# A hybrid attention block on eight cores: a build-time list scheduler in place of program order, fixed rings and stage barriers

## The chip, the cores and the metric

One Trainium2 chip, eight cores, two dies of four cores each. The program runs on all eight at once; every core takes two of the sixteen batch elements, so no core talks to another. The metric is device time in microseconds (us) of the slowest core. The executions here fall in two states: fast, or slow, when the cores of one die (or both) show a lower granted TensorE clock and the time is longer.

## The reference, cut to what matters

One transformer layer over 2048 latent tokens and 256 context tokens, width 1024. Its pieces, in the order in which data flow:

```python
# D=1024, SEQ=2048, CTX=256, batch 16 (2 per core), one layer
sh1, sc1, g1, sh2, sc2, g2 = adaln(c, w_ada, b_ada)      # silu(c) @ w_ada: 1024 x 6144, fp32, 24 MB
hc = modulate(rms_norm(ctx), sh1c, sc1c)                 # "norm 1", context tokens
hx = modulate(rms_norm(x),   sh1,  sc1)                  #           latent tokens
# one combined input projection, cut into q, k, v | gla q, k, v, gate | low-rank decays | merge gates
# softmax attention: 8 query heads, 2 KV heads, QK-norm, rotary; 2304 keys
attn = softmax(q k^T) v
# gated linear attention (GLA): 4 heads, dk=128, dv=256, forward and backward scan
#   S_t = diag(a_t) S_{t-1} + k_t^T v_t ;  o_t = q_t S_t   (chunked; the kernels use chunks of 128)
gla = rms_norm(o_fwd + o_bwd) * silu(gate)
x = x + g1 * (sigmoid(ga) * (attn @ wA) + sigmoid(gb) * (gla @ wG)) @ w_out   # merge, output projection
x = x + g2 * swiglu(modulate(rms_norm(x), sh2, sc2))                          # norm 2, FFN, d_ff 2816
```

GLA and attention both read `hx` and don't depend on each other. The two batch elements of a core are independent throughout. Within a batch element, the FFN of one group of 512 tokens needs nothing of the other groups. This is the freedom that the change sets out to use.

## The kernel before

The kernel issues its instructions in program order. A small class follows who wrote and read each tile and puts the semaphore waits in; stages are walled off by barriers, and buffers come from fixed rings.

```python
def barrier(self):                       # every engine waits for all engines and all DMAs
    sps = [(E.sem, E.cnt) for E in self.E.values() if E.cnt > 0]
    sps += [(o.dsem, o.dcnt) for o in self.dsems]
    for E in self.E.values():
        for sem, val in sps:
            ...
            E.h.wait_ge(sem, val)

class Ring:                              # buffer i of n, in turn
    def next(self):
        it = self.items[self.i % len(self.items)]
        self.i += 1
        return it

# --- stage order, for each of the two batch elements (cut) ---
# adaLN (once) | norm 1 | 4 GLA heads, one after the other | K, V | 32 attention tiles | merge
#              | output projection + norm 2 | FFN, two halves of 1024 tokens      -- S.barrier() between stages
```

One GLA head is projections first, scan after. The forward scan's step, per chunk of 128 tokens:

```python
def core(n):
    S.op("act", lambda e: e.copy(out=Sbf, in_=s32_), ...)
    def mmo(e):                                          # four matmuls per chunk
        e.matmul(pso[:, 0:256], lhsT=qeT[:, 0, tok], rhs=Sbf, start=True, stop=False)
        e.matmul(pso[:, 0:256], lhsT=ATs[:, 0, tok], rhs=gv[:, i, :], start=False, stop=False)
        e.matmul(pso[:, 0:256], lhsT=qeT[:, 1, tok], rhs=SBst[:, n, :], start=False, stop=False)
        return e.matmul(pso[:, 0:256], lhsT=ATs[:, 1, tok], rhs=gv[:, i, :], start=False, stop=True)
    if n < 15:
        state_step(i, 0, first=False)                    # line 828: the state's matmul, then DVE
    S.op("pe", mmo, ...)                                 # lines 861 to 864
def norm(n):
    ...                                                  # Square, Ln, Exp on ACT; scale on DVE (line 877)
    def trs(e):                                          # lines 882, 883: fp32 transposes
        e.transpose(pst[:, 0:128], go[:, 0:128], ident)
        return e.transpose(pst[:, 128:256], go[:, 128:256], ident)
for n in range(18):
    if n < 16: core(n)
    if 0 <= n - 1 < 16: norm(n - 1)
    if 0 <= n - 2 < 16: evac(n - 2)
```

An attention tile (one head, 512 queries) runs nine pairs of key blocks: two score matmuls of 512 columns into a pair of PSUM banks, one Exp of 1024 columns on ACT, eight matmuls with V of 129 columns into an accumulator of two banks. At its end:

```python
pTv = pO2.bitcast(BF16).rearrange("p (a b) -> p a b", a=4)[:, :, 384:512]   # inside the accumulator's banks
S.op("dve", lambda e: e.reciprocal(out=rz, in_=pOv[:, :, 128]), ...)
S.op("dve", lambda e: e.tensor_tensor(out=on, in0=pOv[:, :, 0:128], in1=rz..., op=ALU.mult), ...)
def fin():
    S.op("pe", trs, reads=[on_k, cst_k], writes=pO2_k)                      # four transposes into pTv
    S.op("dve", lambda e: e.tensor_copy(out=aoT[...], in_=pTv), reads=pO2_k, ...)
```

## Time and profile before

| | before |
|---|---|
| time, median of 15 runs | 3715.21 us (3709.83 to 4145.19) |
| PE busy, mean granted clock (profiled core) | 85%, 0.935 |
| stage windows in which PE is far from full, batch 0 | start 195 us; GLA 476; K and V 72; attention 384; output projection with norm 2 110; batch 1's norm 63 |
| stage windows in which PE is full | merge 223; FFN 462 |

The page's line on the chain that ended last (the work followed back from the last instruction to whatever released it) gives PE 73% of the span; all the rest is time in which the end of the program depends on something else than a matmul.

```profile
PE 73%; ACT 7%; DVE 7%; issue 7%; DMA 4%; DVEq 0%; SPq 0%; ACTq 0%; POOLq 0%; POOL 0%
```

Three windows of the stages that the prediction rests on and doesn't show; the columns are start:end, then span, busy time and count for PE, PEld, DVE, ACT, POOL, granted clock, DMA share, GB/s.

```profile
195.00:671.00 476.00, 366.37 (x2956) 251.42 (x2976) 253.40 (x520) 241.00 (x636) 7.25 (x13) 0.88 0.10 15
671.00:743.00 72.00, 46.94 (x262) 27.36 (x268) 37.83 (x61) 23.84 (x46) 2.13 (x4) 0.88 0.20 44
743.00:1127.00 384.00, 335.21 (x3202) 219.20 (x3262) 153.08 (x250) 318.17 (x378) 3.17 (x6) 1.00 0.03 6
```

They are the four GLA heads, K and V, and attention of batch 0. In the first two no engine is above 77%, and the clock granted to TensorE is 0.88, where attention has 1.00: in these windows the emptier stages also have the lower clock. In attention ACT stands at 318 of 384 us.

### The profile page before, as it was taken

What the parts mean: (1) busy time and instruction counts of PE and PEld (TensorE: products, weight loads), DVE (VectorE), ACT (ScalarE), POOL (GpSimd) and SP (SyncE); (2) the same over time, 40 slices, a digit from 0 to 9 for tenths busy, and PEclk for the clock granted to TensorE, in tenths of its full rate; (3) what the DMA queues carried; (4) which work ended last, traced back from release to release, by engine and by line L of the source; (5) the groups of instructions that cost most, each with busy time, mean ns of one, the idle gap of its engine ahead of it and who ended that gap; (6) DMA issues with size and microseconds to landing.
All of it is one profiled execution on the core that took longest, in us unless ns stands there. A gap on an engine that the chain in (4) does not pass through costs nothing.

```text
span 3708.8 us, 58054 instructions; the slowest of 8 cores (3686.3 to 3708.8 us)
## 1 busy us (share of the span) xinstructions
PE 3144.1 (85%) x20290; PEld 1735.4 (47%) x20606; DVE 1407.9 (38%) x2448; ACT 1504.7 (41%) x2696; POOL 207.3 (6%) x382
## 2 busy tenths in 40 slices
PE   7587778688889977999977777868888998799999
PEld 1265445355554433444435455534555443344444
DVE  0244565544342334222224565554444232512212
ACT  0335555388882114101104554547888411411010
POOL 0000000000000001201100000000000000121110
PEclk9698888999999998999987888989999999899999
DMA  9401110100002246844442111010000123584452
GB/s 273 128 8 21 21 21 7 35 7 7 7 1 35 40 103 159 128 92 89 63 126 83 21 21 21 7 32 7 7 7 4 24 41 68 165 149 81 101 78 82
DMA packets 91317, 219.49 MB, mean 59 GB/s; under 512 B 8533, under 2 KB 15065, under 8 KB 89497
## 3 DMA queue, kind: packets, MB, share of 16 engines
q0 software_dynamic: 62624, 133.32, 20.3%
q1 hardware_dynamic: 28410, 82.44, 7.6%
q8 instruction: 172, 2.82, 0.3%
q14 instruction: 111, 0.91, 0.1%
HBM read 281.92 MB, written 33.55 MB: 85 GB/s over the span
## 4 chain that ended last, share of the span: by engine, by line
PE 73%; ACT 7%; DVE 7%; issue 7%; DMA 4%; DVEq 0%; SPq 0%; ACTq 0%; POOLq 0%; POOL 0%
PE ps L1270 8%; PE ps L1277 8%; PE ps L1299 8%; PE ps L1154 6%; PE ps L1147 6%; PE ps L1045 5%; PE ps L1072 5%; PE ps L939 4%; ACT sb_arenaB L1056 4%; PE ps L738 4%; PE ps L751 3%; PE ps L772 3%; PE ps L1210 3%; DVE sb_arenaB L836 2%; PE ps L410 2%
## 5 line engine op out<-in xcount | busy, mean ns | idle before, releaser
L1056 ACT ACTIVATE sb_arenaB<-ps 128x1024 bf16<-128x1024 f32 x576 | 564.5, 1028 | 9.0 <-PE ps L1045 8.1
L1072 PEld LDWEIGHTS ps<-sb_arenaB 128*128 128x128 bf16 x4608 | 302.4, 97 | 167.0 <-issue 45.3
L1045 PE MATMUL ps<-sb_arenaB 128*128 128x512 bf16 x1026 | 314.3, 378 | 77.7 <-ACT sb_arenaB L1056 72.0
L1072 PE MATMUL ps<-sb_arenaB 128*128 128x129 bf16 x4608 | 354.5, 220 | 16.2 <-DVE sb_arenaA L1093 15.6
L1281 ACT ACTIVATE sb_arenaB<-ps 128x512 f32<-128x512 f32 x176 | 105.1, 597 | 647.4 <-PE ps L1270 647.4
L1270 PE MATMUL ps<-sb_hxT,sb_wbuf 128*128 128x512 bf16 x1376 | 332.4, 382 | 9.6 <-issue 8.1
L1277 PE MATMUL ps<-sb_hxT,sb_wbuf 128*128 128x512 bf16 x1382 | 331.2, 380 | 1.4
L1282 DVE TENSOR_TENSOR sb_arenaA<-ps,sb_arenaB 128x512 bf16<-128x512 f32 x176 | 121.8, 692 | 509.4 <-PE ps L1277 494.5
L1299 PE MATMUL ps<-sb_arenaB,sb_arenaA 128*128 128x512 bf16 x1380 | 303.1, 379 | 1.5
L1147 PE MATMUL ps<-sb_hxT,sb_wbuf 128*128 128x512 bf16 x1000 | 240.4, 380 | 3.6 <-DVE sb_arenaA L1093 2.4
L1154 PE MATMUL ps<-sb_arenaA,sb_wbuf 128*128 128x512 bf16 x1006 | 241.2, 381 | 0.9
L1159 ACT ACTIVATE sb_arenaB<-ps 128x512 f32<-128x512 f32 x128 | 76.4, 597 | 358.6 <-PE ps L1147 244.9
L1270 PEld LDWEIGHTS ps<-sb_hxT,sb_wbuf 128*128 128x128 bf16 x1408 | 138.1, 98 | 175.5 <-issue 11.1
L1277 PEld LDWEIGHTS ps<-sb_hxT,sb_wbuf 128*128 128x128 bf16 x1408 | 137.9, 98 | 167.3 <-issue 1.8
L1299 PEld LDWEIGHTS ps<-sb_arenaB,sb_arenaA 128*128 128x128 bf16 x1408 | 137.6, 98 | 166.3
L836 DVE SCALAR_TENSOR_TENSOR sb_arenaB<-sb_arenaB,ps 128x256 f32<-128x256 f32 x256 | 122.8, 481 | 104.0 <-PE ps L828 80.9
L508 PE MATMUL ps<-sb_ident_bf,sb_arenaB 128*128 128x128 bf16 x544 | 61.1, 288 | 115.0 <-DVE sb_arenaB L494 85.7
L1154 PEld LDWEIGHTS ps<-sb_arenaA,sb_wbuf 128*128 128x128 bf16 x1024 | 100.4, 98 | 122.0 <-issue 2.0
L1147 PEld LDWEIGHTS ps<-sb_hxT,sb_wbuf 128*128 128x128 bf16 x1024 | 100.0, 98 | 122.9 <-issue 2.6
L939 PE MATMUL ps<-sb_hxT,sb_wbuf 128*128 128x512 bf16 x630 | 155.9, 393 | 1.0 <-issue 0.7
L968 DVE TENSOR_TENSOR sb_arenaB<-sb_arenaB 128x512 bf16<-128x512 f32 (+1 forms) x84 | 57.1, 679 | 223.8 <-ACT sb_arenaB L967 222.8
L828 PE MATMUL ps<-sb_arenaB,sb_arenaA 128*128 128x256 bf16 x272 | 93.4, 349 | 44.5 <-DVE sb_arenaB L836 37.0
(161 smaller groups left out, 4188.1 us busy)
## 6 DMA issues: line engine op xcount, KB each, us to landing
sb_wbuf<-wfi POOLq DMA_DIRECT2D x176, 256.0 KB, 4.9
out<-sb_arenaA POOLq DMA_DIRECT2D x64, 512.0 KB, 5.0
sb_arenaA<-w_ada SPq DMA_DIRECT2D x12, 2048.0 KB, 18.1
sb_wbuf<-wb POOLq DMA_DIRECT2D x68, 256.0 KB, 3.9
sb_arenaB<-x SPq DMA_DIRECT2D x32, 512.0 KB, 9.4
sb_arenaA<-x SPq DMA_DIRECT2D x32, 512.0 KB, 5.7
sb_arenaA<-out SPq DMA_DIRECT2D x32, 512.0 KB, 4.2
sb_arenaB<-wfo POOLq DMA_DIRECT2D x22, 512.0 KB, 8.3
```

The lines of the kernel that those rows point to most:

```text
L738: last = e.matmul(ps[:, k * 256:(k + 1) * 256], lhsT=hsrc(i0 + k, kt)[0], rhs=wa[:, kt, 128:384], start=(kt == 0), stop=(kt == KT - 1))
L836: S.op("dve", lambda e: e.scalar_tensor_tensor(out=new, in0=old, scalar=dlx[:, dr, i:i + 1], in1=pu[:, 0:256], op0=ALU.mult, op1=ALU.add), ...
L939: last = e.matmul(ps[:, 0:nn], lhsT=w[:, kt, :], rhs=rhs, start=(kt == 0), stop=(kt == KT - 1))
L1045: last = e.matmul(pS[:, u * 512:(u + 1) * 512], lhsT=kT[:, gg, j * 128:(j + 1) * 128], rhs=qTx, start=True, stop=True)
L1056: S.op("act", lambda e, pS=pS, PT=PT: e.activation(out=PT, in_=pS, func=AF.Exp, scale=ATT_SCALE, bias=-ATT_SHIFT), reads=pS_k, writes=[PT_k])
L1072: last = e.matmul(pOv[:, qt, 0:129], lhsT=PT[:, u * 512 + qt * 128:u * 512 + (qt + 1) * 128], rhs=Vt[:, 2 * j + g, 0:129], start=(j == 0 a ...
L1147: last = e.matmul(pG, lhsT=wg[:, kt, :], rhs=hxT[:, kt, c * 512:(c + 1) * 512], start=(kt == 0), stop=(kt == KT - 1))
L1154: last = e.matmul(pY, lhsT=wy[:, kt, :], rhs=src[:, kt, c * 512:(c + 1) * 512], start=(kt == 0), stop=(kt == KT - 1))
L1270: last = e.matmul(pA, lhsT=wa_j[:, kt, :], rhs=hxT[:, kt, c * 512:(c + 1) * 512], start=(kt == 0), stop=(kt == KT - 1))
L1277: last = e.matmul(pB, lhsT=wb_j[:, kt, :], rhs=hxT[:, kt, c * 512:(c + 1) * 512], start=(kt == 0), stop=(kt == KT - 1))
L1282: S.op("dve", lambda e, pB=pB, sa=sa, j=j, cl=cl: e.tensor_tensor(out=uT[:, j, cl * 512:(cl + 1) * 512], in0=pB, in1=sa, op=ALU.mult), rea ...
L1299: last = e.matmul(pF, lhsT=uT[:, j, tl * 128:(tl + 1) * 128], rhs=WoG[:, j, cc * 512:(cc + 1) * 512], start=(j == 0), stop=(j == NJ - 1))
```

## The change

Its intent is that the order of the instructions is no longer the order of the program text. Work is written as tasks (Python generators) that yield operations and requests for SBUF space, PSUM banks or conditions. When the program is built, a list scheduler with a cost model picks, again and again, the ready operation with the smallest (estimated start + priority), and takes buffers from one 184 KB arena and eight PSUM banks as they come free. On the chip nothing is dynamic: each engine still runs one fixed sequence. At the same time the arithmetic of adaLN and of GLA is reorganised. The diff has 1325 added and 1118 removed lines; its core, with cuts marked `...`:

```diff
-    def barrier(self):
-        sps = [(E.sem, E.cnt) for E in self.E.values() if E.cnt > 0]
 ...
+class Machine:
+    def _start(self, op):                       # alternatives (DVE or ACT for a copy): the earlier end wins
 ...
+            late = 0.0
+            if table is not None and table != E.table:
+                late = 1.3                      # price of an activation-table switch
+            if best is None or t + late + cost < best[2]:
+                best = (t, alt, t + late + cost, late)
 ...
+            self.dma_free = max(self.dma_free, E.free) + op.dma[1] / 190e3     # DMA model: 190 GB/s
 ...
+    def run(self):
 ...
+                key = max(t, self.now - 1.0) + task[0] + 0.5 * late
+                if best is None or key < best[0]:
+                    best = (key, task)

 # adaLN: 24 slices of 256 columns, outputs in four 32-partition strips
+            for kt in range(KT):
+                q = kt % 4
+                last = e.matmul(ps.ap[32 * q:32 * q + 32, 0:256], lhsT=scT.ap[:, kt, :], rhs=wa.ap[:, kt, :],
+                                start=(kt < 4 and kt > 0), stop=(kt >= 4))
 ...
+    lane([t_ada(n) for n in range(8)], 3, -2.0, "ada")
+    mod1 = lambda: ada_done[0] >= 8             # norm 1 needs only 8 of the 24
 ...
+    lane([t_ada(n, lambda n=n: att0[0] >= (n - 8) * 1.6) for n in range(8, 24)], 1, 0.3, "adb")  # under attention 0

 # GLA: a head may begin when half of the head before the last is out; no token-major K projection
+        def head_gate(h):
+            return lambda: h < 2 or out_done[h - 2] >= 4
 ...
-                        last = e.matmul(ps[:, k * 128:(k + 1) * 128], lhsT=hsrc(i, kt)[0], rhs=wa[:, kt, 0:128], ...)
+                        last = e.transpose(pv[:, dr, k * 128:(k + 1) * 128], keT.ap[:, dr, k * 128:(k + 1) * 128], ident_bf)
 ...
+                yield dve(lambda e: e.copy_predicated(out=Av, mask=maskp.ap..., data=v1), ...)   # two masked matrices into one
 ...
-                    e.matmul(pso[:, 0:256], lhsT=qeT[:, 0, tok], rhs=Sbf, start=True, stop=False)
-                    e.matmul(pso[:, 0:256], lhsT=ATs[:, 0, tok], rhs=gv[:, i, :], start=False, stop=False)
-                    e.matmul(pso[:, 0:256], lhsT=qeT[:, 1, tok], rhs=SBst[:, n, :], start=False, stop=False)
-                    return e.matmul(pso[:, 0:256], lhsT=ATs[:, 1, tok], rhs=gv[:, i, :], start=False, stop=True)
+                    e.matmul(out, lhsT=qe.ap[:, 0, o:o + 128], rhs=X["Sf"][n].ap, start=True, stop=False)
+                    e.matmul(out, lhsT=A.ap[:, o:o + 128], rhs=v.t.ap[:, n % 2, :], start=False, stop=False)
+                    last = e.matmul(out, lhsT=qe.ap[:, 1, o:o + 128], rhs=X["Sb"][n].ap, start=False, stop=True)

 # attention: the end of a tile transposes into a bank of its own
-        pTv = pO2.bitcast(BF16).rearrange("p (a b) -> p a b", a=4)[:, :, 384:512]
+            ev_fin[ti].set()                    # accumulator free: the division is done
+            pt = yield Bank(1)
+            ptv = pt.ap.bitcast(BF16)[:, 0:512]

 # FFN: a group of 512 tokens starts when its own norm 2 is done
+        def t_f(Hh, j, cl):
+            c = 2 * Hh + cl
+            yield Wait(ev_h2[c])

 # batch 1: later priority, may begin with the second half of batch 0's FFN, within a space reserve
+    g1, att0, left0 = batch(0, 0.0, lambda: True, None)      # g1: f_started >= 1
+    M.reserve = lambda: left0() + 56 * 4
+        batch(1, 3.0, g1, None)
```

## The prediction

> **What bounds the kernel now.** I read the page's head and its forty slices, then the busy times by stage, then the chain of waits inside one attention tile.
>
> The page:
>
> ```profile
> span 3708.8 us, 58054 instructions; the slowest of 8 cores (3686.3 to 3708.8 us)
> PE 3144.1 (85%) x20290; PEld 1735.4 (47%) x20606; DVE 1407.9 (38%) x2448; ACT 1504.7 (41%) x2696; POOL 207.3 (6%) x382
> ...
> PE   7587778688889977999977777868888998799999
> DVE  0244565544342334222224565554444232512212
> ACT  0335555388882114101104554547888411411010
> ...
> PEclk9698888999999998999987888989999999899999
> ```
>
> TensorE is the bound, but only in two kinds of stage (merge, FFN: nines). The low PE digits stand where ACT and DVE are high, and ACT and DVE are nearly empty where PE is full: work that could lie side by side lies one after the other. The stage windows (start:end, then span, busy time and count for PE, PEld, DVE, ACT, POOL, granted clock, DMA share, GB/s):
>
> ```profile
> 37.00:136.00 99.00, 96.50 (x230) 22.79 (x230) 9.34 (x22) 4.68 (x8) 0.00 (x0) 0.91 0.55 167
> 136.00:195.00 59.00, 15.64 (x144) 14.39 (x144) 26.04 (x49) 30.26 (x57) 1.78 (x4) 0.56 0.75 192
> 225.00:283.00 58.00, 52.14 (x437) 37.95 (x442) 29.27 (x55) 32.36 (x59) 1.60 (x3) 1.00 0.02 4
> 283.00:330.00 47.00, 26.85 (x142) 14.87 (x143) 31.91 (x73) 25.31 (x96) 0.00 (x0) 0.74 0.23 36
> 1350.00:1460.00 110.00, 74.73 (x378) 35.92 (x384) 55.01 (x81) 42.71 (x73) 10.53 (x19) 0.83 0.59 168
> 1460.00:1922.00 462.00, 455.91 (x2069) 206.97 (x2112) 105.16 (x152) 53.82 (x89) 61.52 (x112) 0.99 0.55 97
> 1922.00:1985.00 63.00, 16.15 (x144) 14.74 (x144) 27.22 (x49) 30.25 (x57) 3.73 (x7) 0.51 0.67 189
> ```
>
> These are adaLN, norm of batch 0, projections and scan of one gated-linear-attention (GLA) head, output projection with norm 2, FFN of batch 0, norm of batch 1. The FFN does 2112 matmuls of 512 columns in 462 us, hence the 0.2158 us each at which eight take 1.726 us start to start in the timeline; 256 columns take 0.110, 128 take 0.0558. I call this streaming time: the busy time counts pipeline depth too (mean 380 ns), so 85% flatters.
>
> Streaming time of one batch, counted from the loops and these three prices: norm 1 8.0; low-rank 15.6; GLA 4 x 74.4 = 298; attention's K and V 33; attention 32 x 10.2 = 326; merge 1024 x 0.2158 = 221; output projection 55 and norm 2 7; FFN 456. Sum 1420. Twice that, plus adaLN's fp32 matmuls and broadcast, about 106 (timeline: 6.96 us for eight of 512 columns, 14 us of broadcast), is 2945. So 3709 - 2945 = 764 us pass in which TensorE streams nothing. By stage: start to 195 us: 81; each GLA (476 us) 163; each K/V stage (72) 39; each attention (about 384) 58; each output projection and norm 2 (110) 48; norm of batch 1 55; small change elsewhere.
>
> Inside attention the chain of waits shows a tile of 12.1 us:
>
> ```profile
> 904.85 0.64 ACT sb_arenaB L967
> 905.49 0.92 ACT sb_arenaB L1056
> 906.42 0.35 issue
> ...
> 908.51 1.74 PE ps L939 x8
> 910.25 0.02 issue
> ...
> 910.34 0.04 ACT sb_arenaB L951
> 910.38 0.45 issue
> 910.83 1.03 ACT sb_arenaB L1056
> ```
>
> ACT has nine Exp at 0.985 us back to back (four in 3.94) plus Square 0.60, Ln 0.59 and Exp 0.64, about 10.8; PE streams 10.2. ACT binds, and loses some 1.3 us per tile at its end, where the transposes and their copy use the accumulator's own banks and hold the next PV matmuls.
>
> [...] granted clock 1.00 in dense projections, 0.74 in the scan, 0.51 and 0.56 in the norms. [...] Here the FFN ran dense on eight cores at 0.99[...], though one of the three timed runs took 4119.92 us. [...] The page here has 1283 ns on every ACT_TABLE_LOAD, so interleaving Silu with Exp and Ln has a price per switch.
>
> **The change part by part.** It replaces program order, fixed buffer rings and the barriers between stages by a list scheduler: tasks with priorities, buffers taken from one arena and PSUM banks by need, copies given to ACT or DVE, weights streamed ahead. All of it is decided when the program is built; on the chip each engine still runs one fixed order.
>
> Less streaming. Low-rank: both directions in one 64-column matmul, 15.6 to 7.8. GLA per head: token-major K projection gone (-8.0) but its context columns go through the feature-major one (+0.9); decay matmuls of one kind instead of two (-2.0); transposes of ke added (+2.0); the two masked matrices merged, so three matmuls instead of four per chunk (-1.7); output transposes bf16 instead of fp32 (-2.4). 74.4 becomes about 63.2, four heads 253. Per batch 1420 - 7.8 - 45 = 1367; both 2734. AdaLN: 24 slices of 256 columns in four strips; one unpacked fp32 256-column matmul would be 0.435, eight 3.5; [...] New streaming sum 2794, so 151 less.
>
> Less emptiness, 764 before:
> - Start. Only 8 of 24 MB of adaLN weights stand before norm 1, and x loads beside them. At the first window's 251 GB/s, 8 MB plus 3 MB of inputs is some 44 us; with latency the GLA starts near 57, not 195. The other 16 slices go under attention. Empty time 81 to 50.
> - GLA of batch 0. Scan of one head lies beside projections of the next, no ring of two. Busy demand per head: PE 63; ACT 18.9 for four fused 1024-wide Exp/Ln per chunk, 13 for 32 scaled states, 9 squares, 8 for the rest, near 49; DVE 5.4 + 5 + 5.5 + 16 + 8 + copies, near 54. Three engines at about 80% each in strict order will not reach 100%: I take 83% PE. 261 + 8 at 83% leaves 55 empty, not 163.
> - K/V: overlapped with the last scan, but attention waits for all of GLA: 10 left of 39, for each batch.
> - Attention: own bank for the transposes, so the accumulator is free after the 0.18 + 0.69 us of division. ACT floor 10.8. A 1.73 us query projection or an adaLN slice still slips in front of a score matmul. I take 11.4 us: 38 empty of 58 in each batch.
> - Output projection/norm 2: the FFN starts on the first 512 tokens while the rest is projected, no barrier and 1 MB weight wait (the chain had 17.2 us of DMA there): 12 left of 48, twice.
> - Batch 1's norm and GLA: allowed from the second half of batch 0's FFN, arena permitting. The FFN has ACT 0.12 and DVE 0.23 busy, so what fits costs only PE time. The arena reserve will hold much of GLA until the FFN's last third: 163 + 55 become 50.
> - FFN, merge, tail: about 24.
> Sum: 50 + 55 + 20 + 76 + 24 + 50 + 24 = 299. Time 2794 + 299 = 3093. Since every hole is also taken with cost guesses that look close (0.69 us for a 512-wide DVE op, as in the trace), I round towards the better side: 3075 us, 17% less.
>
> **The rivals.**
> 1. TensorE-bound all through: batch 1 vanishes under the FFN, GLA reaches 95%. For it: ACT and DVE have room on average (41%, 38%). Against: attention's ACT floor alone leaves 19 us per batch, and the start can't go. About 2930.
> 2. Order paid on the chip: greedy choice puts long PE blocks (3.5 us for a value pair or a gate pair) before short critical ones, Silu/Exp switches multiply (8 loads at one line now; 30 to 60 more at 1.3 us or so), PSUM's 8 banks stall the pipelines, weight loads queue behind POOL's copies in strict order. GLA stays at 70% and attention at 12.1: +70 +45 +60, about 3250.
> 3. [...] Against: the FFN at 0.99. I give it 5%.
> 4. Nothing hidden because DMA or the buffers bind: DMA stands at 28%, bursts of 0.8 in the FFN; batch 1 finds no arena until the FFN ends: 3150.
>
> **Range and chances.** The streaming cut (151) and the start (some 30 of emptiness) hardly depend on scheduling: 3530 already, over 2% faster. The range goes from rival 1 to rival 2 without their extremes: 2950 to 3230. Faster 0.97, same 0.02, slower 0.01.
>
> **What would show it.** First GLA matmul near 57 us; attention beginning near 400 instead of 740; tiles of 11.4 us and ACT above 90% there; scan and projections mixed, with clock above 0.95 instead of 0.88; merge 220 and FFN about 456 plus whatever batch 1 puts in between; batch 1's norm inside FFN 0 and no window at clock 0.5; PE busy above 90%. I am wrong in mechanism if those stages keep their lengths, if the batch-1 GLA runs alone at its old 476 us, or if attention lengthens under the adaLN slices; wrong in size if GLA's PE share is far from 83%.

The text is as recorded, but for passages that are cut, each marked: figures and mechanisms that no trace or run of this case shows. The sum holds a cut term: new streaming came to 2794, which is 2734 for the two batches and, for the rest, adaLN's 24 slices, whose price is cut; 2794 + 299 = 3093, put down as 3075. The 151 of less streaming, 2945 - 2794, holds that term too. At the 2.0 us of PE that a slice took under attention in the changed kernel (see below), the 24 would be 48 us and the saving 163 (an estimate); this document goes on with 151. Rival 3 said that the dense stages would run at a lower clock in most executions. The busy demands per head are estimates from counts and the mean times of like operations in the trace before (0.404 us for a scaled state, 1.05 for an activation of 1024 columns).

## The result, and the profile after

| | before | after |
|---|---|---|
| median | 3715.21 us (15 runs) | 3130.32 us (12 runs) |
| range | 3709.83 to 4145.19 | 3125.65 to 3580.81 |
| fast runs over fast runs | | 0.8421 (0.8403 to 0.8438) |

The ratio is the mean time of one kernel's fast runs over that of the other's of the same rounds, so it isn't quite the ratio of the medians. Nine of the twelve runs of the changed kernel were fast, with a mean of 3129.7 us; in the slowest, 3580.81, the cores of one die had a granted clock of 0.812 to 0.817 and those of the other 0.977 to 0.979. Below, a time of a kernel is the mean of its fast runs, and a difference is taken to 3129.7. The output is right.

The changed kernel's page: the span, the busy times, and four of the rows of forty slices.

```profile
span 3132.5 us, 55526 instructions; the slowest of 8 cores (3106.4 to 3132.5 us)
...
PE 2926.7 (93%) x19780; PEld 1649.5 (53%) x19780; DVE 1279.1 (41%) x2142; ACT 1522.0 (49%) x2436; POOL 219.4 (7%) x428
...
PE   4989879999999999999989997899999997999999
...
DVE  1565674444333452221235657644432325422222
ACT  1787768888711132101137787698883112310110
...
PEclk9999889999999999999999998999999998999999
```

Set them beside the rows in the prediction. The PE row has nines where it had fives to sevens; what is left are the start (4), the end of each batch's GLA (the first two sevens, at 392 to 470 and 1879 to 1958 us) and the output projection of batch 1 (the third, at 2584 to 2663 us, where PE is busy for 62.6 of 79 us; a wait for its weights, shown below, comes just before and reaches into it). PE's busy time fell by 217 us and DVE's by 129, ACT's rose by 17. Mean granted clock rose from 0.935 to 0.977 on the profiled cores. The chain that ended last is now

```profile
PE 83%; ACT 7%; issue 4%; DVE 3%; DMA 3%; SPq 1%; DVEq 0%; ACTq 0%; POOL 0%; POOLq 0%
```

so PE's share went from 73% to 83%. The stage windows of the changed kernel's slowest core (columns as above; the fifth is a stretch inside the third):

```profile
0.00:37.00 37.00, 5.74 (x36) 2.32 (x40) 1.77 (x9) 1.88 (x3) 5.11 (x13) 1.00 0.97 196
37.00:84.00 47.00, 32.55 (x206) 17.73 (x199) 9.93 (x24) 16.36 (x33) 0.00 (x0) 1.00 0.69 216
84.00:466.00 382.00, 332.81 (x2771) 238.72 (x2768) 239.12 (x435) 282.94 (x587) 26.64 (x63) 0.94 0.15 34
140.00:340.00 200.00, 185.72 (x1660) 140.77 (x1658) 116.48 (x214) 161.56 (x306) 17.32 (x40) 0.97 0.10 16
340.00:440.00 100.00, 77.71 (x559) 49.15 (x560) 69.04 (x138) 69.02 (x194) 4.28 (x15) 0.88 0.18 38
466.00:852.00 386.00, 378.77 (x3637) 240.94 (x3637) 163.66 (x283) 329.54 (x388) 6.35 (x12) 0.99 0.19 51
852.00:1064.00 212.00, 212.00 (x987) 96.25 (x986) 63.47 (x93) 37.93 (x63) 16.06 (x29) 1.00 0.32 48
1064.00:1198.00 134.00, 123.35 (x645) 59.55 (x644) 73.67 (x114) 48.35 (x78) 12.15 (x22) 0.96 0.67 165
1198.00:1612.00 414.00, 410.96 (x1920) 187.72 (x1919) 99.28 (x147) 55.83 (x97) 46.69 (x86) 1.00 0.54 110
1612.00:1990.00 378.00, 334.11 (x2796) 240.89 (x2793) 240.45 (x437) 287.11 (x589) 29.79 (x65) 0.93 0.15 38
1990.00:2372.00 382.00, 357.65 (x3324) 228.07 (x3325) 155.65 (x261) 332.20 (x390) 6.36 (x12) 0.99 0.06 10
...
2573.00:2720.00 147.00, 129.70 (x655) 61.24 (x654) 74.60 (x115) 48.69 (x78) 13.15 (x24) 0.93 0.73 168
```

They are: two parts of the start, GLA with K and V, the middle of GLA, the tail of the last head, attention 0, merge 0, output projection with norm 2 and the first FFN work, FFN 0, GLA with K and V of batch 1, attention 1, and the passage to the FFN of batch 1. GLA with K and V takes 382 us (378 in batch 1) and took 476 + 72 = 548. From the GLA's first projection to the start of attention, PE is busy 87% of the time and was 75% (413.31 of 548). The borders are set by eye, to some 10 us: the first score matmul of attention 1 comes only at 1999.7, and from it to PE's last work for attention pass 368 us, where the kernel before took 387 (739.4 to 1126.2). Merge, 212 and 201, is bound by streaming in both kernels (PE busy for all of the 212 and 201 us, and for 219.92 of 223 in the kernel before).

The chain in order of time, from the last long wait of the start on (start us, us, what; "DMA" is time in which the chain waits for a transfer):

```profile
22.49 30.25 DMA sb_arena<-w_ada
...
52.99 1.03 PE ps L678 x2
54.02 1.91 PE ps L682 x16
...
56.01 0.38 ACT sb_arena L583
...
56.52 0.99 PE ps L698 x4
57.51 0.99 PE ps L678 x2
58.50 1.91 PE ps L682 x16
```

GLA can't begin before adaLN's first eight slices are through. The chain waits for a slice's weights until 52.7 us; the chain has 30 us for that transfer, while x tiles and GLA weights come in beside it. Five slices are then still to be done, and they come 4.5 us apart: each is one short chain on PE, the bias's matmul (line 678, 0.99 us), the eight packed ones (line 682, 1.91), a copy on ACT, and two small fp32 matmuls that turn the result (line 698, 0.99).

The clock has a part in this that the windows hide. The trace has no clock record before 84.6 us, and the windows count time without a record as 1.00; the spacing of the matmuls says otherwise. Here are the packed eight of a slice and the 128-column bf16 transposes of norm 1 in the start, and then the packed eight of a slice under attention:

```profile
72.03 1.94 PE L682 MATMUL ps<-sb_arena,sb_scT 128*32 128x256 f32 x16
75.51 3.57 PE L756 MATMUL ps<-sb_cstb,sb_arena 128*128 128x128 bf16 x32
```

```profile
474.05 1.07 PE L682 MATMUL ps<-sb_arena,sb_scT 128*32 128x256 f32 x16
```

The transposes follow each other at 0.107 us where the prediction has 0.0558, and the same packed work takes 1.94 us instead of 1.07: until its first clock record the core runs at about half rate. Under attention the three PE steps of a slice take about 0.54 + 1.0 + 0.50 = 2.0 us, in the start 3.9, so of the 22 us that the five slices take, some 9 are the clock (an estimate from these spacings). In the kernel before, where the matmuls of adaLN are dense, the record has the full clock, 1.00, from 22.5 us on.

Two more pieces of the same chain, later:

```profile
384.12 16.75 DMA sb_arena<-wav
...
2573.16 23.61 DMA sb_arena<-wo
```

Here two weight loads hold up everything, 16.75 us before the values of attention (`wav`) and 23.61 us before batch 1's output projection (`wo`). The program lets the first begin when the last GLA head's projections are done, and the second when six of eight parts of the merge are.

### The profile page after: what moved, and what is told of

Same layout as the page of the kernel before. It is cut to its first block, busy times and chain, and to the rows that moved or that the text cites. A ratio compares the mean times of both kernels' runs of the same rounds, so it can differ in the third digit from the quotient of the medians.

```text
span 3132.5 us, 55526 instructions; the slowest of 8 cores (3106.4 to 3132.5 us)
## 1 busy us (share of the span) xinstructions
PE 2926.7 (93%) x19780; PEld 1649.5 (53%) x19780; DVE 1279.1 (41%) x2142; ACT 1522.0 (49%) x2436; POOL 219.4 (7%) x428
## 3 DMA queue, kind: packets, MB, share of 16 engines
q1 hardware_dynamic: 28784, 116.19, 11.4%
## 4 chain that ended last, share of the span: by engine, by line
PE 83%; ACT 7%; issue 4%; DVE 3%; DMA 3%; SPq 1%; DVEq 0%; ACTq 0%; POOL 0%; POOLq 0%
PE ps L1455 19%; PE ps L1485 10%; PE ps L1282 8%; PE ps L1346 7%; PE ps L1354 7%; PE ps L1308 7%; PE ps L989 4%; PE ps L893 4%; PE ps L1018 3%; PE ps L1399 3%; ACT sb_arena L1294 3%; PE ps L1223 2%; PE ps L756 1%; PE ps L1197 1%; DMA sb_arena<-w_ada 1%
## 5 line engine op out<-in xcount | busy, mean ns | idle before, releaser
L1455 PE MATMUL ps<-sb_arena 128*128 128x512 bf16 x2816 | 613.5, 379 | 0.0
L1294 ACT ACTIVATE sb_arena<-ps 128x1024 bf16<-128x1024 f32 x576 | 558.8, 1022 | 8.8 <-PE ps L1282 4.9
L1455 PEld LDWEIGHTS ps<-sb_arena 128*128 128x128 bf16 x2816 | 275.3, 98 | 331.4 <-issue 0.6
L1459 ACT ACTIVATE sb_arena<-ps 128x512 f32<-128x512 f32 x176 | 104.9, 597 | 635.1 <-PE ps L1455 635.0
L1308 PEld LDWEIGHTS ps<-sb_arena 128*128 128x128 bf16 x4608 | 303.3, 97 | 134.0 <-issue 11.8
L1282 PE MATMUL ps<-sb_arena 128*128 128x512 bf16 x1152 | 341.8, 378 | 20.2 <-ACT sb_arena L1294 15.9
L1308 PE MATMUL ps<-sb_arena 128*128 128x129 bf16 x4608 | 354.5, 220 | 3.2 <-DVE sb_arena L1243 1.5
L1485 PE MATMUL ps<-sb_arena 128*128 128x512 bf16 x1408 | 305.9, 379 | 1.0 <-DVE sb_arena L1488 1.0
L1460 DVE TENSOR_TENSOR sb_arena<-ps,sb_arena 128x512 bf16<-128x512 f32 x176 | 121.6, 691 | 426.6 <-PE ps L1455 422.3
L1358 ACT ACTIVATE sb_arena<-ps 128x512 f32<-128x512 f32 x128 | 76.4, 597 | 365.9 <-PE ps L1346 297.5
L1346 PE MATMUL ps<-sb_arena 128*128 128x512 bf16 x1024 | 241.9, 379 | 0.0
L1354 PE MATMUL ps<-sb_arena 128*128 128x512 bf16 x1024 | 241.9, 379 | 0.0
L1485 PEld LDWEIGHTS ps<-sb_arena 128*128 128x128 bf16 x1408 | 137.8, 98 | 167.7 <-issue 2.4
L1354 PEld LDWEIGHTS ps<-sb_arena 128*128 128x128 bf16 x1024 | 100.1, 98 | 120.3
L1346 PEld LDWEIGHTS ps<-sb_arena 128*128 128x128 bf16 x1024 | 100.1, 98 | 119.9
L1062 DVE SCALAR_TENSOR_TENSOR sb_arena<-sb_arena,ps 128x256 f32<-128x256 f32 x256 | 116.8, 476 | 108.7 <-PE ps L1052 102.1
L1071 ACT ACTIVATE sb_arena<-sb_arena 128x256 bf16<-128x256 f32 x256 | 124.4, 504 | 51.5 <-DVE sb_arena L1062 44.1
L989 PE MATMUL ps<-sb_arena 128*128 128x256 bf16 x1152 | 139.1, 276 | 0.0
L893 PE MATMUL ps<-sb_arena 128*128 128x512 bf16 (+1 forms) x576 | 137.8, 391 | 0.8 <-DVE sb_arena L1488 0.8
```

The lines of the kernel that those rows point to most:

```text
L893: last = e.matmul(ps.ap[:, 0:W], lhsT=w.ap[:, kt, :], rhs=hxc.ap[:, kt, :], start=(kt == 0), stop=(kt == KT - 1))
L989: last = e.matmul(ps.ap[:, k * 256:(k + 1) * 256], lhsT=hxc.ap[:, kt, o + k * 128:o + (k + 1) * 128], rhs=w.ap[:, kt, :], start=(kt == 0), ...
L1062: yield dve(lambda e: e.scalar_tensor_tensor(out=R2.ap, in0=R.ap, scalar=dl.ap[:, dr, prev:prev + 1], in1=ps.ap[:, 0:256], op0=ALU.mult, o ...
L1071: yield Op([("act", lambda e: e.activation(out=St.ap, in_=R.ap, func=AF.Copy, scale=dcol), act_cost(256, False) + 0.09, None)], [R, dl], [St])
L1282: last = e.matmul(pS.ap[:, u * 512:(u + 1) * 512], lhsT=kT[g].ap[:, j * 128:(j + 1) * 128], rhs=q.ap, start=True, stop=True)
L1294: yield act(lambda e: e.activation(out=PT.ap, in_=pS.ap, func=AF.Exp, scale=ATT_SCALE, bias=-ATT_SHIFT), act_cost(1024), [pS], writes=[PT] ...
```

## The experiments

Theory. Of the 585 us, some 151 is streaming that is no longer done; the rest is overlap in four places, each with its own wait removed (head behind head in GLA, adaLN behind attention, FFN behind norm 2, batch 1 behind FFN 0), and finer order inside the stages. Put back one of those waits and its share returns. Rival A: the overlap between stages is worth little, and the gain is streaming and the clock. Rival B: the heads hardly overlap, since three engines in strict order fill one head already. Twelve kernels ran.

### One wait put back at a time

**The heads of GLA, one after the other** (run a).

```diff
-            return lambda: h < 2 or out_done[h - 2] >= 4
+            return lambda: h < 1 or out_done[h - 1] >= 8
```

> The changed kernel, but a GLA head may only start when the one before it is finished (one gate changed). Theory A (the time came from work lying side by side): the scan and output of each head are exposed again; a head, about 86 us now for some 63 us of matmul streaming, takes 100 to 110 us, so +110 to +190 us for the eight heads, all of it between the first GLA matmul and the first score matmul of each batch. Rival B (the time came from the smaller amount of matmul work): the work is untouched, so under +20 us.

Measured: the two fast runs are 3267.8 and 3268.8 us, ratio to the kernel before 0.8797 (0.8742 to 0.8851), so 139 us more than with the change. Four of six runs were slow, the profiled one among them, on one die only:

```profile
die 0 (median of its cores): 3264.5 us, clock 0.950
die 1 (median of its cores): 3331.3 us, clock 0.926
```

The other die's median, 3264.5, is that of a fast run; only its cores were read. There each head takes about 100 us (the value projections come in bursts at 80, 200, 300 and 400 us), and attention begins at 530 instead of 466. So overlap of heads is worth about 70 us per batch. Rival B falls.

**All of adaLN ahead of norm 1** (run b).

```diff
-    lane([t_ada(n) for n in range(8)], 3, -2.0, "ada")
-    mod1 = lambda: ada_done[0] >= 8
+    lane([t_ada(n) for n in range(24)], 3, -2.0, "ada")
+    mod1 = lambda: ada_done[0] >= 24
 ...
-    lane([t_ada(n, lambda n=n: att0[0] >= (n - 8) * 1.6) for n in range(8, 24)], 1, 0.3, "adb")
```

> The changed kernel with all 24 adaLN slices before the first norm, none under attention. Theory A: 16 MB more at some 240 GB/s stand in front of the GLA, about +66 us at the start, and attention of batch 0 gets back the 20 us by which its tiles are longer than those of batch 1 (386 against 367 us): +45 us in all. Rival B: the slices cost PE and DMA wherever they lie, so under +15 us.

Measured: 3181.3, 3185.7 and 3203.1 us, ratio 0.8586 (0.8531 to 0.8640): 60 more by the mean, 56 by the median, somewhat more than expected. The expectation's 240 GB/s was an estimate; it lies between the 216 of the changed kernel's start and the 251 of the first window before. Its chain has the slices 4.5 to 6.6 us apart, all through the start, and this start too runs at about half rate, up to its first clock record at 167 us: the packed eight take 1.91 us in every slice of the chain, and 1.00 in the chain of the changed kernel under attention. There the same slice costs about 1 us in all, as will be seen below. Sixteen times the difference is 56 at least; of it some 30 are the clock (16 x 1.9 us, an estimate), and the rest falls to the holes in a slice's chain.

**The FFN waits for all of norm 2** (run c).

```diff
-            yield Wait(ev_h2[c])
+            yield Wait(lambda: all(e_.on for e_ in ev_h2))
```

> The changed kernel, but the FFN waits until all four 512-token groups have been through norm 2. Theory A: output projection and norm 2 have holes again, as in the kernel before (36 us of PE not busy in 110): +20 to +30 us for each batch, +50 in all. Rival B: under +15 us.

Measured: 3158.7, 3165.5 and 3168.8 us, ratio 0.8517 (0.8475 to 0.8559): 35 more for the two batches, and less than I expected.

**Batch 1 waits for the end of FFN 0** (run d).

```diff
-        return (lambda: f_started[0] >= 1), att_i, ...
+        return (lambda: fo_done[0] >= 16), att_i, ...
```

> The changed kernel, but batch 1 may start only when batch 0 is finished. My prediction took some 170 us of batch 1's front as hidden under batch 0's FFN; the trace shows batch 1's first transposes only at about 1580 us, 32 us before the FFN's last matmul, and the GLA of batch 1 then takes as long as that of batch 0. Theory A': the overlap that exists is worth only the norm and first loads, +20 to +40 us. Rival: the overlap does more than the trace shows, +100 us or more.

Measured: 3140.4 to 3145.3 us in four fast runs, ratio 0.8458 (0.8419 to 0.8497): 13 more. The overlap of the two batches is worth almost nothing, less than half of what I had by then come to expect.

**All four together** (run e; the edits of a, b, c and d).

> All four gates at once: heads one after the other, all adaLN first, FFN after all of norm 2, batch 1 after batch 0: the new work and buffers in the old order of stages. If the four losses are separate things they add: +135, +55, +35, +13 on 3130, about 3370. If they share holes, less: 3300. What is then left to the kernel before (about 340 us) is the 151 us of matmul streaming removed and whatever the finer order inside stages gives.

Measured: 3383.1 and 3385.3 us (four of six runs slow), ratio 0.9114 (0.9067 to 0.9161): 254 more than the change as it is. The four single costs add to 139 + 60 + 35 + 13 = 247, so they are nearly independent. What is then left, 3712.8 - 3384.2 = 329 us, is the other half of the result: the streaming that went, and order inside the stages. Three windows of this run's slowest core show where: the four GLA heads, what is left of K and V, and attention of batch 0.

```profile
170.00:578.00 408.00, 325.02 (x2597) 233.11 (x2596) 211.90 (x392) 280.75 (x540) 35.53 (x70) 0.82 0.13 31
578.00:612.00 34.00, 27.61 (x181) 16.72 (x179) 31.12 (x49) 20.42 (x45) 0.00 (x0) 1.00 0.00 1
612.00:978.00 366.00, 344.33 (x3217) 220.62 (x3216) 152.72 (x255) 321.86 (x379) 6.35 (x12) 0.99 0.06 10
```

By these windows GLA takes 408 us for 476, K and V 34 for 72, attention 366 for 384; their borders are not quite at the same places in both kernels. By the first and last matmuls of each stage, batch 0 takes from its first low-rank matmul to its first FFN matmul 133 us less (GLA with K and V 90, attention 18, output projection 29, merge 4 more), batch 1 127 less; the gap from FFN 0 to batch 1's low-rank matmuls is 30 us and was 66, and GLA begins 29 us earlier. That is 133 + 127 + 35 + 29 = 324, which covers the 329. Of it, by the prediction's count, 151 are streaming; the rest, some 180, is what is left for the order inside the stages. That is a remainder and not a measurement: only attention's accumulator was tried by itself (run h), and the clock's share was not separated. Rival A is still wrong in the main: the four overlaps alone are 254 of 585 measured us, and streaming is 151 by the count.

### The pieces inside the stages

**fp32 output transposes back in the changed kernel** (run f). The change turns two fp32 transposes per chunk into bf16 ones; I took them as pure streaming.

```diff
-            go = yield alloc([128, 2, 256], BF16, name="go")
+            go = yield alloc([128, 2, 256], F32, name="go")
 ...
-                        last = e.transpose(ptv[...], go.ap[:, u, hf * 128:(hf + 1) * 128], ident_bf)
+                        last = e.transpose(ptv[...], go.ap[:, u, hf * 128:(hf + 1) * 128], cst.ap[:, 0, :])
```

> The changed kernel with the GLA output transposed in fp32 again (256 transposes; in the trace before, the next matmul starts 0.13 and 0.11 us after one in fp32 and 0.056 us after one in bf16) and its eviction at 0.69 instead of 0.42 us. Theory (GLA of the changed kernel is matmul-bound at 79%): the 16 us of streaming cost +8 to +20 us. Rival (holes absorb it): under +4 us.

Measured: 3145.1, 3146.2 and 3146.4 us (the other four of seven were slow), ratio 0.8472 (0.8438 to 0.8506): 16 more. The trace has the loss in the right place: over all eight cores GLA with K and V takes 392 and 411 us (batch 0 and 1, first value projection to first score matmul) instead of 379 and 399, and the stages after it some 7 us less. The edit also makes the copy out of PSUM slower (0.69 us instead of 0.42 on DVE), so the matmuls alone are not shown to be the cause.

**The same piece put into the kernel before** (run g).

```diff
-        go_r = ring(2, [128, 256], F32, "go")
+        go_r = ring(2, [128, 256], BF16, "go")
 ...
-                    e.transpose(pst[:, 0:128], go[:, 0:128], ident)
+                    e.transpose(pv_[:, 0:128], go[:, 0:128], ident_bf)        # pv_ = pst.bitcast(BF16)
```

> The kernel before with only this piece of the change: the GLA output in bf16, transposed in bf16. In its scan PE waits 0.76 us in every chunk of 1.72 us for the DVE product in front of these transposes. If that chain sets the chunk, taking 0.12 us of streaming from PE per chunk gives the 16 us only where the transposes are themselves in the loop: -5 to -16 us. Rival (less matmul work explains the gain): at least the same saving as in the changed kernel and more from the DVE, -20 us or more.

Measured: 3706.4, 3714.3 and 3718.1 us (five of eight runs slow) against 3712.8 before, ratio 0.9997 (0.9944 to 1.0051). My expectation missed. The times alone can't tell 0 from -16, as the interval is 20 us wide to each side, but the trace shows where the saving went. PE's timeline in the scan (start us, us, engine, line, what, and in brackets the idle time before it and who ended it), in the kernel before:

```profile
661.57 0.30 PE L882 MATMUL ps<-sb_cst,sb_arenaB 128*128 128x128 f32 x1 [0.76 <-DVE sb_arenaB L877]
661.71 0.27 PE L883 MATMUL ps<-sb_cst,sb_arenaB 128*128 128x128 f32 x1
661.82 0.27 PE L828 MATMUL ps<-sb_arenaB,sb_arenaA 128*128 128x256 bf16 x1
...
663.29 0.30 PE L882 MATMUL ps<-sb_cst,sb_arenaB 128*128 128x128 f32 x1 [0.76 <-DVE sb_arenaB L877]
```

and in run g, on a core of the undisturbed die:

```profile
650.00 0.22 PE L883 MATMUL ps<-sb_ident_bf,sb_arenaB 128*128 128x128 bf16 x1 [0.83 <-DVE sb_arenaB L877]
650.05 0.22 PE L884 MATMUL ps<-sb_ident_bf,sb_arenaB 128*128 128x128 bf16 x1
650.11 0.27 PE L828 MATMUL ps<-sb_arenaB,sb_arenaA 128*128 128x256 bf16 x1
...
651.93 0.22 PE L883 MATMUL ps<-sb_ident_bf,sb_arenaB 128*128 128x128 bf16 x1 [1.11 <-DVE sb_arenaB L877]
```

The first transpose of all 128 chunks on the same two cores, before and in run g (busy us, mean ns, then PE's idle time in front of them):

```profile
L882 PE MATMUL ps<-sb_cst,sb_arenaB 128*128 128x128 f32 x128 | 41.8, 327 | 91.4 <-DVE sb_arenaB L877 91.4
L883 PE MATMUL ps<-sb_ident_bf,sb_arenaB 128*128 128x128 bf16 x128 | 31.4, 245 | 75.8 <-DVE sb_arenaB L877 75.8
```

In the kernel before, the two transposes start 0.14 and 0.11 us ahead of what follows them, with bf16 0.05 to 0.06. The chunks come 1.76 us apart on average before, and 1.69 in run g (1.58 to 1.93 in the stretch shown; all eight cores before, the four of the undisturbed die in g), and PE waits for DVE's scaling (line 877) 0.60 us per chunk instead of 0.70. So the saving does reach the scans: the eight of them, first to last transpose, take 202 us instead of 212. But the granted clock in them fell from 0.88 to 0.71, and the rest of the two GLA stages, to the first score matmul, took 880 us instead of 869, at a clock of 0.857 instead of 0.874. Outside of GLA nothing changed (2616 and 2619 us). The slow die is not the cause: in run g's three fast runs the cores' mean clock is 0.910 to 0.927, in the fast runs of the kernel before in the same rounds 0.925 to 0.938. What the scans gained, the slower clock took back; why it falls is not shown here. In the changed kernel GLA is dense (PE busy 87%, clock 0.94 in batch 0), and there the edit is worth 16 us, copy included.

**Attention's transposes back in the accumulator's banks** (run h).

```diff
-            ev_fin[ti].set()
-            pt = yield Bank(1)
-            ptv = pt.ap.bitcast(BF16)[:, 0:512]
+            ptv = pO.ap.bitcast(BF16).rearrange("p (a b) -> p a b", a=4)[:, :, 384:512]
 ...
+            ev_fin[ti].set()                      # only after the copy
```

> The changed kernel with the attention transposes again in the accumulator's own banks, which are free only after the copy. Theory: the tile of 11.4 us goes back toward 12.1: +0.5 to +0.7 us for each of 64 tiles, +30 to +45 us. Rival (the tile is bound by the ACT order and PE, the own bank gives nothing): under +8 us.

Measured: 3159.1 and 3159.8 us, and 3201.8 with two cores of one die at a clock of 0.96; ratio with all three 0.8547 (0.8484 to 0.8609). The two close ones are 30 more than the change as it is. The tile shows it directly. One reciprocal ends each tile; in batch 1's attention, which has no adaLN slices in it, DVE's timeline has in the changed kernel

```profile
2103.00 0.18 DVE L1241 RECIPROCAL sb_arena<-ps 128x4 f32<-128x4 f32 x1 [4.55 <-PE ps L1308]
...
2114.39 0.18 DVE L1241 RECIPROCAL sb_arena<-ps 128x4 f32<-128x4 f32 x1 [4.12 <-PE ps L1308]
```

and in run h

```profile
2104.85 0.18 DVE L1241 RECIPROCAL sb_arena<-ps 128x4 f32<-128x4 f32 x1 [5.04 <-PE ps L1306]
...
2116.84 0.18 DVE L1241 RECIPROCAL sb_arena<-ps 128x4 f32<-128x4 f32 x1 [5.02 <-PE ps L1306]
```

so about 11.4 us per tile against 12.0. Over the 31 steps of a batch it is 11.42 against 11.92 in batch 1 and 11.94 against 12.36 in batch 0, and 32 x 0.50 + 32 x 0.42 = 29 us, just what was measured. The tile of the kernel before is 12.05, so the bank of its own gives 0.50 of the 0.63 us: the step of the prediction on attention is confirmed by itself.

### What holds the rest, and a version that beats both

**A smaller reserve of the arena for batch 1** (run i). Does the space that is kept free stop batch 1 from running under FFN 0?

```diff
-    M.reserve = lambda: left0() + 56 * 4
+    M.reserve = lambda: left0()
```

> The changed kernel without the arena reserve that holds batch 1 back (56 KB of 184 KB; only the room that the FFN's own products still need stays reserved). If the reserve is what keeps batch 1's GLA out of batch 0's FFN, it starts some 100 us earlier and the time falls by 60 us or more. If the FFN's weights and products (44 KB each, with 16 KB of inputs) fill the arena anyway, as I now think, batch 1 gets its norm and first loads in, then stands: within 20 us of 3130.

Measured: 3115.0 to 3122.9 us, ratio 0.8411 (0.8391 to 0.8432): 10 less. The first value projection of batch 1 now comes 190 us earlier, but it is a single group. PE's timeline has it here in this run, and then in the changed kernel (each on its slowest core):

```profile
1408.92 3.30 PE L989 MATMUL ps<-sb_arena 128*128 128x256 bf16 x16
```

```profile
1599.74 3.23 PE L989 MATMUL ps<-sb_arena 128*128 128x256 bf16 x16
```

After it, run i has none until about 1630 us. By the scheduler's own record the arena is full by then, if the room that the FFN's products will still need is counted: at most 7 of 184 KB per partition are free for batch 1 until the FFN's last tiles. The FFN's weights and its products take 44 KB each, and inputs, streams and batch 1's first loads the rest. So with the reserve gone the space still holds batch 1. An arena larger by more than a few KB can't be tried (one of 192 KB no longer builds), and the question how much a GLA truly under the FFN would bring stays open.

**A faster guess for the DMA in the cost model** (run j).

```diff
-            self.dma_free = max(self.dma_free, E.free) + op.dma[1] / 190e3
+            self.dma_free = max(self.dma_free, E.free) + op.dma[1] / 250e3
```

> The changed kernel, the scheduler being told 250 GB/s for DMA instead of 190 (the first window of the trace before moved 251). Nothing else changes but the order that follows from it. Theory: the order is sensitive to this only where it puts loads and the work that waits for them, so a few per cent of the 338 us that PE does not stream: 0 to -30 us. Rival (wrong cost guesses are what keeps PE from 95%): -60 us or more.

Measured: 3117.8, 3121.6 and 3122.9 us, ratio 0.8415 (0.8390 to 0.8439): 9 less. Nothing changes on the chip but the order that comes out of the build.

**Also looser gates** (run k: run j, and heads one step earlier, two gate projections and three output projections in flight).

```diff
-            return lambda: h < 2 or out_done[h - 2] >= 4
+            return lambda: h < 2 or out_done[h - 2] >= 2
 ...
-        lane([t_g(h, q) for h in range(NH) for q in range(4)], 1, PR - 0.4, "g_")
+        lane([t_g(h, q) for h in range(NH) for q in range(4)], 2, PR - 0.4, "g_")
 ...
-        lane([t_wo(i) for i in range(16)], 2, PR + 0.2, "wo_")
+        lane([t_wo(i) for i in range(16)], 3, PR + 0.2, "wo_")
```

> Four loosened limits together: 250 GB/s in the scheduler's estimate, the third head may start when the first has half its outputs waited for now (2 instead of 4), two gate-projection tasks at once instead of one, three output-projection tiles at once instead of two. Theory (what is left between 3130 and the streaming sum is mostly holes in GLA and around norm 2): GLA 10 to 20 us shorter per batch, norm 2 some 10 us per batch: -30 to -70 us. Rival (PSUM's eight banks and the arena set these stages): within 15 us.

Measured: 3084.4, 3086.8 and 3087.8 us, ratio 0.8321 (0.8286 to 0.8357): 43 less.

**Priorities found by a search in the scheduler's own estimate** (run l). The estimated end of the program comes out of the build, without a chip. A random search over ten priorities and limits kept what lowered it. Of the edit on top of run k (the rest alike):

```diff
-        lane([t_v(h, p) ...], 2, PR - 0.2, "v_")
+        lane([t_v(h, p) ...], 2, PR - 0, "v_")
-            lane([t_o(h, p) ...], 2, PR - 0.4, ...)
+            lane([t_o(h, p) ...], 2, PR - 0.6, ...)
-                    M.add(t_fin(ti, pO), PR - 0.5, "fin%d" % ti)
+                    M.add(t_fin(ti, pO), PR - 0.1, "fin%d" % ti)
-        wo = WStream("wo", ..., lambda: m_done[0] >= 6, True, uses=16)
+        wo = WStream("wo", ..., lambda: m_done[0] >= 4, True, uses=16)
-    M.reserve = lambda: left0() + 56 * 4
+    M.reserve = lambda: left0() + 24 * 4
```

> The loosened kernel with ten priorities and limits more, found by a random search over the scheduler's own estimate of its end (3171 for the changed kernel at 250 GB/s, 3119 for the loosened one, 3093 for this; the chip had 3123 and 3087 for the first two). If the estimate orders variants rightly and the ratio of about 0.99 holds, 3060 to 3070. If a gain of 26 us in it is noise of the estimate, 3087 plus or minus 10.

Measured: 3049.4 to 3052.0 us in five fast runs (one slow, 3152.4), ratio 0.8224 (0.8208 to 0.8240): 79 less than the change, faster than both kernels, and better than the 3060 to 3070 that I expected. Its page:

```profile
span 3050.4 us, 55210 instructions; the slowest of 8 cores (3033.1 to 3050.4 us)
...
PE 2866.8 (94%) x19469; PEld 1640.2 (54%) x19780; DVE 1278.9 (42%) x2138; ACT 1492.2 (49%) x2409; POOL 224.5 (7%) x432
...
PE   4999879999999999999999997899999998999999
```

The estimates of the build were 3304 (the change), 3171 (run j), 3119 (k) and 3093 (l); the chip gave 3130, 3121, 3086 and 3051. The model ranks them rightly, though its size of a step is off: it promised 133 us for run j, whose order was worth 9; the edit makes the model's own transfers faster, which changes nothing on the chip. Between the last three, which share a model, 78 estimated stand against 70 measured.

One caution holds for all of these runs: any edit makes the scheduler reorder the whole program. Differences of some 10 us (d, i, j) may be the luck of an order and not the worth of the edit; the intervals of their ratios overlap that of the change itself, and that of run f (16 us) touches it. The runs were spread over several chips, each with the kernel before beside it.

## Why the prediction was right or wrong, point by point

The time, 3130 against 3075, lay in the range, and the mechanism was mostly as told. The sum of the terms was 3093; rounding it "towards the better side" moved it away from the result. Step by step:

- **Less streaming, 151.** Never measured alone, but the matmuls of the two traces, counted by line at these prices, give about 2930 and 2790 us, some 140 less (an estimate; the trace before lacks some records). The eight matmuls of an adaLN slice take 1.07 us under attention, at a clock of 0.99, and 1.94 at the half rate of the start. Without packing eight of 256 columns would take 3.48 us, half of the 6.96 that eight of 512 take in the kernel before; four strips thus gave 3.48 / 1.07 = 3.3 times (an estimate from these two times).
- **Start.** Failed in size: the first value projection of GLA came at 83.6 us, not 57. The 11 MB were about right, but came at some 200 GB/s (196 in the first 37 us, 216 after) and not at 251, so the last wait for weights ended at 52.7 us and not at 44. After it I had 13 us; five slices at 4.5 us on PE's own chain and 8.5 us of norm and low-rank followed. I had priced a slice by its streaming and not by the length of its chain, and at the full clock, where the start ran at about half of it: 0.107 us from transpose to transpose against 0.0558.
- **GLA of batch 0.** Streaming 253 + 8 + 8 of low-rank and norm, with K and V's 33, is 302 us; it passed in 382. That is 79%, where I took 83% for the GLA and added 10 for K and V. The 80 us left empty, against 65, lie at the end: from 340 to 440, when the last head has no other to overlap with, PE is busy 78% at a clock of 0.88, and the chain has the 16.75 us wait for `wav` there. Between 140 and 340 it is 93%.
- **Attention.** The tile is as said: 11.42 us over batch 1's 31 steps from the first reciprocal, 2012.38, to the last, 2366.46; 11.94 in batch 0, where the sixteen slices cost about 1 us each ((11.94 - 11.42) x 31 / 16), less than the price that is cut: they take some 2.0 us of PE each, and about half of that falls in holes (an estimate). I had 364 us without slices (32 x 11.4), and with them the price of sixteen on top; from the first score matmul to PE's last work there, 368 without and 386 with them were measured. "ACT above 90%" is wrong, at 85 and 87% of the windows: some 1.1 us per tile ACT waits for the ones-matmul of the QK-norm, which the fixed order of ACT puts in front of the next Exp.
- **Output projection and norm 2.** Right in kind: run c gives 35 us for starting the FFN by groups, about half of the 72 that I had taken off with all else there. In batch 1 the wait for `wo`, 23.6 us, came back.
- **Batch 1's norm and GLA.** This is the step that failed in mechanism. I let 163 + 55 become 50 because that GLA would run under FFN 0. It doesn't: its first value projection comes at 1599.7 us and FFN 0 ends with a matmul at about 1614; batch 1's GLA with K and V takes 386 us from there to its first score matmul, as batch 0's takes 384. Run d puts the overlap at 13 us. What shrank the emptiness is the denser stage itself and a shorter gap. From the end of merge 0 to the start of attention 1 some 110 to 120 us are empty, where my terms had 78. Rival 4 named the right cause for this step, the arena (not the DMA), and its number, 3150, lies nearer to the measured 3130 than my 3075.
- **The rivals.** 1 (2930) fell with GLA at 79%. 2 (3250): the table loads did multiply, from 25 to 85 of 1283 ns each, yet every stage with ACT in it got shorter or stayed, and attention's tile is at 11.4. 3 (most executions at a lower clock) fell: in the profiled run all eight cores ran the window of FFN 0 at a granted clock of 0.99 to 1.00, and nine of twelve runs were fast; slow runs exist for both kernels (3580.81 us, and 4119.92 before).
- **The sum.** Non-streaming time is about 3130 - 2800 = 330 against 299: start +10, GLA and K/V +15, merge 0 to attention 1 +32 to +42, attention 0 with its slices -18 (against a count that holds their price), the rest small; these terms are read from windows to within some 10 us and are not a closed balance.

Left open: how the order inside the stages divides beyond attention's 30 us; how much of the gain is the clock itself, and why it was lower with bf16 transposes in the kernel before (0.71 in the scans of run g against 0.88); what a GLA under the FFN would be worth with space for it.

## What to carry to other kernels

Before counting on one stage hiding under another, count the space that both need at the same time: here ACT and DVE had room for the next batch (busy for 13 and 24% of FFN 0's 414 us), and its buffers were taken. Overlap neighbours that share a stage's buffers first (head behind head, token group behind token group); these were worth 139 and 35 us, batch under batch 13. A cut in the bound engine's work need not show in the time: the same transposes were worth 16 us in the dense kernel and nothing measurable in the sparse one, where they shortened the scans by 10 us and the granted clock in them fell from 0.88 to 0.71. So put the clock of a stage beside its length before and after a cut, and where a trace has no clock record yet, read the rate from the spacing of equal matmuls (0.107 us against 0.0558 here). On this one example it paid to order first and trim after, and then to let the scheduler's own estimate search for the priorities.
